# Half 1's last feed-forward tile issued product by product between matmuls of half 0's second product

## The chip, the cores and the metric

One Trainium2 chip, one of its cores. The metric is the device time of one execution in microseconds (us), the median of several runs.

## The reference, cut to what matters

One step of a hybrid decoder trunk in f32: a half-step SwiGLU feed-forward, a token mixer (pooling, Mamba-2), a second half-step feed-forward and a norm. 1024 prompt tokens and 64 sample tokens share all weights; D_MODEL is 1024, D_FF 2816.

```python
def swiglu(x, w_in, w_out):
    gu = x @ w_in
    g, u = gu[..., :D_FF], gu[..., D_FF:]
    return (jax.nn.silu(g) * u) @ w_out

x = x + 0.5 * swiglu(rmsnorm(x, norm_ffn1), ffn1_w_in, ffn1_w_out)
...
x = x + 0.5 * swiglu(rmsnorm(x, norm_ffn2), ffn2_w_in, ffn2_w_out)
```

## The kernel before

**Halves and tiles.** The tokens are worked on in two halves: half 0 has 512, half 1 has 576 (`NTOK`, line 31). A feed-forward's first product makes the hidden layer in 22 tiles of 128 rows (`NFF`). A hidden tile of a half is stored to DRAM (`hd0` to `hd21` in a trace, for each half) and reloaded for the second product, which makes eight output tiles `po` per half out of all 22.

**Split numbers.** f32 is multiplied as a sum of products of rounded parts. ACT writes the rounded part of a tile, DVE subtracts it from the tile and writes the rest; the page's "split" is such a pair. For a weight they are `wh` (L457) and `wl` (L458), for a reloaded hidden tile `hh` or `hp` (L353) and `hr` or `hp` (L355). TensorE (PE) then does three products of parts for each pair of tiles; for half 0 in the first product it does two, since one wider tile holds both parts of the activations.

**Products of the first half of a feed-forward.** Most hidden tiles are made in Strassen-Winograd form: seven products of half-size blocks in the place of eight. `wino` (L481) runs over `PRODUCTS`, in the order 1, 2, 6, 5, 7, 3, 4. Their weights come from `wino_weights` (L442): four raw blocks a11, a12, a21, a22 (loaded by `wino_raw`, L472, DMA at L477, tag `wraw` with six buffers), and four sums of them, which POOL makes at L451: s1 = a21 + a22, s2 = s1 - a11, s3 = a11 - a21, s4 = a12 - s2. They are split in the order a11, a12, s2, s1, s3, s4, a22, with three buffers each for `wh` and `wl`. What PE has accumulated in PSUM (`pw` in a trace) goes out by `after0` for half 0 (L555 on, with POOL's half sums at L567 and its product at L588) and by `after` for half 1 (L591 on, POOL's product at L618): copies by ACT, sums by DVE, a SiLU by ACT. The next product in a bank waits for the copy of the last.

**The order of the work.** `ffn` (L640) makes the tiles up to `NFF - N_APART` with each weight used for both halves. The last one, tile 21, is made apart: for half 0, then for half 1, each with weights of its own, loaded and split anew (L668 to L670). The second product follows, half 0 first: the 22 hidden tiles are loaded at L685 and split, output tiles 0 and 1 are accumulated together and then the others one by one. In a trace these matmuls are `po<-hh`, `po<-hr` and `po<-hp`. The weights of output tiles 0 and 1 have been split long before and lie in DRAM as halves `part`; `load_w` reloads them at L282 into `wh` and `wl`, every other pair into two of the six `wraw` buffers.

The program text doesn't set the order on the engines alone. A tile scheduler gives each instruction a place by its priority and by a model of durations, and work that runs beside a stream of matmuls is written as a chain: a generator that `start` registers, and that `tick`, called after each group of matmuls, moves on one step when the modelled PE time since its last step has passed the number that it yielded. `finish` runs a chain to its end. What stands in each engine's queue is fixed when the program is built, and each engine works its queue in that order. All loads and stores here are issued by SP (SyncE) from one queue, so that one that waits holds those behind it. PE's matmuls are all at L164.

Of the kernel before, what the change touches and what calls it, by code (L numbers as in the profile page):

```python
# [14 lines left out]
P = 128  # L15
D = 1024
KD = D // P
FF = 2816
# [17 lines left out]
N_ACT, N_PAIR, N_BIG, N_PD = 42, 8, 3, 4  # L36
N_RAW, N_W = 6, 3
N_FX, N_S, N_PDF = 17, 4, 6
N_PLAIN, N_APART = (3, 2), 1

PRODUCTS = (("1", 0), ("2", 1), ("6", 0), ("5", 2), ("7", 0), ("3", 2), ("4", 0))

# [20 lines left out]
def tile_hybrid_pool_ssd_macaron(  # L63
# [71 lines left out]
    def start(gen, delay=0.0):  # L135
        c = Chain(gen, delay)
        chains.append(c)
        return c
# [17 lines left out]
    def tick():  # L156
        while chains:
            c = min(chains, key=lambda q: q.due)
            if c.due > pe[0]:
                return  # L160
            c.step()
# [318 lines left out]

    def wino(weights, nk, xs, after):  # L481


        banks = [[None] * 3 for _ in xs]
        for (p, b), (wh, wl) in zip(PRODUCTS, weights):
            for i, (h, X) in enumerate(xs):
                n = NPAIR[h]
                new = banks[i][b] is None
                if new:
                    banks[i][b] = psum("pd", "pw" + p)  # L490
                out = banks[i][b][:, :n]
                if h == 0:
                    both = banks[i][b].rearrange("p (a b) -> p a b", a=2)
                    for k in range(nk):
                        x = X[p][k]
                        mm(both, wh[:, k, :], x, start=new and k == 0, stop=False, free=True)
                        mm(out, wl[:, k, :], x[:, 0, :], start=False, stop=k == nk - 1, free=True)
                    after(p, i, banks[i])
                    tick()
                    continue  # L500
                for k in range(nk):
                    xh, xl = X[p][k]
                    for j, (W, x) in enumerate(((wh, xh), (wh, xl), (wl, xh))):
                        mm(out, W[:, k, :], x, start=new and k == 0 and j == 0, stop=k == nk - 1 and j == 2, free=True)
                after(p, i, banks[i])
                tick()

    def combine(h, xn, hi, lo, hl, X, pace):

# [38 lines left out]
                X["4"][i] = hl[i][:, :, s_]  # L548
            yield pace

    def ffn_in(wi, ff, xs):

        out = {}

        def after0(p, i, bk):  # L555

            A, B, C = bk
            n = NPAIR[0]
            f, s_ = slice(0, n), slice(n, 2 * n)
            if p == "1":  # L560
                out[i] = o = {"g": fx(name="g"), "t": fx(name="t"), "v": fx(name="v")}
                S.copy(o["t"][:, : 2 * n], A)
                return
            g, t, v = out[i]["g"], out[i]["t"], out[i]["v"]

            def halves(o, x):
                G.tensor_tensor(o, x[:, f], x[:, s_], op=ALU.add)  # L567

            if p == "2":
                V.tensor_tensor(g[:, : 2 * n], B, t[:, : 2 * n], op=ALU.add)  # L570
                halves(g[:, f], g)
                S.activation(g[:, f], g[:, f], AF.Silu)
            elif p == "6":
                S.copy(v[:, : 2 * n], A)  # L574
            elif p == "5":
                S.copy(t[:, : 2 * n], C)
            elif p == "7":
                V.tensor_tensor(t[:, : 2 * n], A, t[:, : 2 * n], op=ALU.add)  # L578
                halves(t[:, f], t)
            elif p == "3":  # L580
                V.tensor_tensor(v[:, : 2 * n], C, v[:, : 2 * n], op=ALU.add)
                halves(g[:, s_], v)
                S.activation(g[:, s_], g[:, s_], AF.Silu)
            else:
                S.copy(t[:, s_], A[:, s_])
                V.tensor_tensor(t[:, s_], A[:, f], t[:, s_], op=ALU.add)
                V.tensor_tensor(g[:, f], g[:, f], t[:, s_], op=ALU.mult)
                G.tensor_tensor(g[:, s_], g[:, s_], t[:, f], op=ALU.mult)  # L588
                dma(hdram[0][ff], g[:, : 2 * n])

        def after(p, i, bk):  # L591
            h = xs[i][0]
            if h == 0:
                return after0(p, i, bk)
            n = NPAIR[h]
            A, B, C = (b[:, :n] if b is not None else None for b in bk)
            if p == "1":
                t = fx(name="t")
                out[i] = o = {"g": fx(name="g"), "t1": t[:, :n], "t5": t[:, :n], "t2": t[:, n : 2 * n]}
                S.copy(o["t1"], A)  # L600
                return
            o = out[i]
            g1, g2 = o["g"][:, :n], o["g"][:, n : 2 * n]
            if p == "2":
                V.tensor_tensor(g1, B, o["t1"], op=ALU.add)
                S.activation(g1, g1, AF.Silu)
            elif p == "6":
                S.copy(o["t2"], A)
            elif p == "5":
                S.copy(o["t5"], C)  # L610
            elif p == "7":
                V.tensor_tensor(o["t5"], A, o["t5"], op=ALU.add)
            elif p == "3":
                V.tensor_tensor(g2, C, o["t2"], op=ALU.add)
                S.activation(g2, g2, AF.Silu)
            else:
                V.tensor_tensor(g1, g1, A, op=ALU.mult)
                G.tensor_tensor(g2, g2, o["t5"], op=ALU.mult)  # L618
                dma(hdram[h][ff], o["g"][:, : 2 * n])

        wino(wino_weights(wi, 0, 4, 4, ff * P, FF + ff * P), 4, xs, after)

    def ffn_in_plain(wi, ff, x):

# [14 lines left out]
    def ffn(wi, wo, prep, after, half=None, side=None):  # L639

        X, todo, behind = [{}, {}], [], []
        for h in HALVES:
            finish(prep[h][0])
            x = prep[h][1][0]
            gen = combine(h, x[3], x[1], x[2], x[4], X[h], T_PACE)

            def first(gen):
                for p in gen:  # L650
                    if p is None:
                        return
                    yield p

            c = start(first(gen), T_AT)
            for ff in range(N_PLAIN[h]):
                ffn_in_plain(wi, ff, x[:3])
            todo.append(c)
            behind.append(start(rest(c, gen)))
        for c in behind:  # L660
            finish(c)
        if side:
            side = start(side, PART_AT)
        for ff in range(N_PLAIN[1], N_PLAIN[0]):
            ffn_in(wi, ff, [(1, X[1])])
        for ff in range(N_PLAIN[0], NFF - N_APART):
            ffn_in(wi, ff, [(h, X[h]) for h in HALVES])
        for h in HALVES:  # L668
            for ff in range(NFF - N_APART, NFF):
                ffn_in(wi, ff, [(h, X[h])])  # L670
        if side:
            finish(side)
        for h in HALVES:
            N = NTOK[h]
            parts = [], []
            for k in range(NFF):

                own = k < 4 if h == 0 else not half and k >= NFF - 2
                if 4 <= k < 4 + N_PAIR and (h == 0 or half):
                    a, t, _ = pair(576, "hp")  # L680
                    t = t.bitcast(F32)
                else:
                    t, a = (fx(d, n_) if own else act((P, 576), d, n_) for d, n_ in ((F32, "hr"), (F32R, "hh")))
                t = t[:, :N]
                dma(t, hdram[h][k])  # L685
                split(t, a[:, :N], t.bitcast(F32R))
                parts[0].append(a)
                parts[1].append(t.bitcast(F32R))
            xt = []
            for ms in ((0, 1),) + tuple((m,) for m in range(2, KD)):  # L690
                po = [banks([(h,)], "pd", "po")[0] for _ in ms]
                for kb in range(0, NFF, 4):
                    n4 = min(4, NFF - kb)
                    for m, pts in zip(ms, po):
                        wh, wl = load_w(wo, kb, n4, m * P)
                        for kk in range(n4):
                            products([pts], wh, wl, kk, slice(0, P), [(h, *parts)], kb + kk, NFF)
                            tick()
                for m, pts in zip(ms, po):
                    x_ = fx(name="x")  # L700
                    dma(x_[:, :N], xspill[h][m])
                    for pt, (a, b) in zip(pts, PIECES[h]):
                        V.scalar_tensor_tensor(x_[:, a:b], pt[:, : b - a], 0.5, x_[:, a:b], op0=ALU.mult, op1=ALU.add)
                    xt.append(x_)
                if half and ms[-1] == KD // 2 - 1:
                    half(h, xt)
            after(h, xt)
# [904 lines left out]
```

## Time and profile before

| | |
|---|---|
| runs | 2926.48, 2932.68, 2932.84 us |
| median of the runs | 2932.68 us |
| profiled execution | 2926.27 us |
| its span | 2924.5 us |
| granted PE clock, mean | 0.998 |
| PE busy | 98% |
| DVE / ACT / POOL busy | 58% / 41% / 18% |
| DMA, mean | 171 GB/s |

The profile shows one execution. Its span runs from the first to the last instruction that it has recorded, and the time of the execution is 1.8 us longer. Rows of the timeline give the start, the duration, the engine, the line, what is written and read, and in brackets the engine's idle time before the instruction and what released it. PE, DVE (VectorE), ACT (ScalarE), POOL (GpSimd) and SP are the engines, PEld is PE's loading of weights. The passage from the first product to the second is at about 495 to 533 us in the first feed-forward and at 2611 to 2649 us in the second.

### The profile page before, as it was taken

The page shows a single profiled execution, that of the slowest core. Times are in us where ns is not written, and L with a number is a line of the kernel's source. Part 1 is how long each engine was busy: PE and PEld are TensorE (multiplying, and loading weights), DVE is VectorE, ACT ScalarE, POOL GpSimd, SP SyncE. Part 2 cuts the span into 40 slices and gives each one's busy share as a digit, 9 for nine tenths or more (in the row PEclk, how much of TensorE's full clock was granted, in tenths as well). Part 3 has the DMA queues.
Part 4 walks back from the last instruction along what each step waited for, and adds up shares of the span by engine and source line. Part 5 has one row for each costly group of instructions (what it writes and reads, how often), then busy time and mean ns, then how long its engine had stood idle before and what let it go on. Part 6 is the DMA issues. An engine that isn't in the chain of part 4 may idle for free.

```text
span 2924.5 us, 50164 instructions
## 1 busy us (share of the span) xinstructions
PE 2873.3 (98%) x18622; PEld 2621.2 (90%) x18622; DVE 1706.2 (58%) x3172; ACT 1208.9 (41%) x2456; POOL 533.3 (18%) x642
## 2 busy tenths in 40 slices
PE   7999999999999999999999999999999999999998
PEld 6999999789988888788999989999999999987898
DVE  6665555434273897787643786867666554453432
ACT  5444444323242655443332554443233444443422
POOL 6444444000000000000000010100035444440000
PEclk9999999999999999999999999999999999999999
DMA  4575554854335878678434566556574532236652
GB/s 135 166 227 181 161 173 131 283 188 145 101 97 164 281 254 265 205 226 280 129 98 148 170 187 185 168 165 186 177 244 154 162 98 78 82 103 210 216 161 73
DMA packets 542266, 501.23 MB, mean 171 GB/s; under 512 B 36388, under 2 KB 391780, under 8 KB 542014
## 3 DMA queue, kind: packets, MB, share of 16 engines
q1 hardware_dynamic: 542006, 498.03, 54.4%
q8 instruction: 146, 2.39, 0.3%
q14 instruction: 98, 0.80, 0.1%
q10 hardware_dynamic: 16, 0.00, 0.0%
HBM read 355.94 MB, written 142.20 MB: 170 GB/s over the span
## 4 chain that ended last, share of the span: by engine, by line
PE 90%; DMA 4%; DVE 3%; ACT 1%; issue 1%; POOL 1%; SPq 0%; POOLq 0%; ACTq 0%; DVEq 0%
PE pw L164 26%; PE po L164 18%; PE pc L164 9%; PE pg L164 8%; PE pz L164 7%; PE pu L164 5%; PE pso L164 5%; PE pbp L164 3%; PE pwo L164 3%; PE pyd L164 1%; PE pst L164 1%; PE pyo L164 1%; DMA bsel<-in_bsel_dram 1%; PE pgm L164 1%; DMA hr<-hd 1%
## 5 line engine op out<-in xcount | busy, mean ns | idle before, releaser
L293 DVE TENSOR_TENSOR wl<-wraw,wh 128x512 fp32r<-128x512 f32 (+1 forms) x416 | 284.4, 685 | 409.2 <-ACT wh L292 396.0
L292 ACT ACTIVATE wh<-wraw 128x512 fp32r<-128x512 f32 (+1 forms) x416 | 257.4, 620 | 617.6 <-PE po L164 248.7
L164 PE MATMUL pw<-X,wh 128*128 128x288 f32 (+1 forms) x1416 | 353.9, 329 | 5.3 <-ACT v L574 3.5
L164 PE MATMUL pw<-X,wl 128*128 128x288 f32 (+1 forms) x936 | 268.6, 287 | 0.0
L164 PEld LDWEIGHTS pw<-X,wh 128*128 128x128 f32 x1416 | 237.6, 188 | 27.3 <-ACT v L574 4.2
L164 PE MATMUL pc<-hl,wh 128*128 128x288 f32 (+1 forms) x1152 | 256.6, 331 | 0.0
L164 PE MATMUL pw<-hl,wh 128*128 128x512 f32 x608 | 219.5, 396 | 1.1 <-DVE t L578 1.0
L458 DVE TENSOR_TENSOR wl<-s,wh 128x512 fp32r<-128x512 f32 x168 | 131.9, 785 | 144.4 <-ACT wh L457 122.8
L164 PE MATMUL po<-hh,wh 128*128 128x288 f32 (+1 forms) x800 | 210.4, 323 | 3.5 <-ACT hh L353 2.5
L164 PE MATMUL po<-hr,wh 128*128 128x288 f32 (+1 forms) x800 | 210.6, 322 | 0.1
L164 PE MATMUL po<-hh,wl 128*128 128x288 f32 (+1 forms) x800 | 210.0, 322 | 0.0
L164 PE MATMUL pg<-hl,wh 128*128 128x288 f32 (+1 forms) x864 | 201.7, 338 | 0.8 <-issue 0.8
L164 PEld LDWEIGHTS pc<-hl,wh 128*128 128x128 f32 x1152 | 184.5, 188 | 18.1 <-issue 3.5
L164 PE MATMUL pw<-hi,wh 128*128 128x288 f32 x640 | 189.1, 296 | 0.6 <-ACT t L610 0.6
L164 PE MATMUL pw<-hi,wl 128*128 128x288 f32 x640 | 188.4, 294 | 0.0
L164 PE MATMUL pw<-lo,wh 128*128 128x288 f32 x640 | 188.4, 294 | 0.0
L164 PEld LDWEIGHTS pw<-X,wl 128*128 128x128 f32 x936 | 176.5, 189 | 0.0
L164 PE MATMUL pz<-hl,wh 128*128 128x288 f32 (+1 forms) x768 | 174.4, 335 | 0.0
L164 PE MATMUL pw<-hl,wl 128*128 128x256 f32 x608 | 169.2, 278 | 0.0
L164 PE MATMUL pc<-hl,wl 128*128 128x288 f32 (+1 forms) x576 | 158.2, 328 | 0.0
L164 PEld LDWEIGHTS pg<-hl,wh 128*128 128x128 f32 x864 | 141.3, 189 | 15.7 <-issue 2.5
L458 DVE TENSOR_TENSOR wl<-wraw,wh 128x512 fp32r<-128x512 f32 x126 | 103.2, 819 | 87.5 <-ACT wh L457 81.0
(375 smaller groups left out, 6872.7 us busy)
## 6 DMA issues: line engine op xcount, KB each, us to landing
wh<-part SPq DMA_DIRECT2D x204, 256.0 KB
wl<-part SPq DMA_DIRECT2D x204, 256.0 KB
wraw<-in_ffn_w_in_dram SPq DMA_DIRECT2D x188, 256.0 KB
wraw<-in_w_in_dram SPq DMA_DIRECT2D x180, 256.0 KB
wraw<-in_ffn_w_out_dram SPq DMA_DIRECT2D x120, 256.0 KB
part<-wh SPq DMA_DIRECT2D x112, 256.0 KB
part<-wl SPq DMA_DIRECT2D x112, 256.0 KB
ab<-acsd SPq DMA_DIRECT2D x64, 256.0 KB
```

Source lines behind the costliest of these rows:

```text
L164: T.matmul(out, lhsT, rhs, start=start, stop=stop, skip_group_check=free)
L292: S.activation(wh, raw, AF.Copy)
L293: V.tensor_tensor(wl, raw, wh.bitcast(F32), op=ALU.subtract)
L458: V.tensor_tensor(wl, a, wh.bitcast(F32), op=ALU.subtract)
```

## The change

Half 0's tile 21 is made as before. Half 1's becomes a chain, `behind`, that is started after it and moves on one product per step while the second product of half 0 is being issued, each step 1.3 us of modelled PE time after the last (`APART_PACE`); what is left of it is issued behind output tiles 0 and 1. For this, `wino` is turned into a generator, `wino_steps`, that yields after each product. The matmuls, splits, sums and transfers are the same in number.

```diff
-N_PLAIN, N_APART = (3, 2), 1
+N_PLAIN, N_APART, APART_PACE = (3, 2), 1, 1.3
...
     def wino(weights, nk, xs, after):
+        for _ in wino_steps(weights, nk, xs, after):
+            tick()
+
+    def wino_steps(weights, nk, xs, after):
...
                     after(p, i, banks[i])
-                    tick()
+                    yield
                     continue
...
                 after(p, i, banks[i])
-                tick()
+                yield
...
-    def ffn_in(wi, ff, xs):
+    def ffn_in(wi, ff, xs, apart=False):
...
-        wino(wino_weights(wi, 0, 4, 4, ff * P, FF + ff * P), 4, xs, after)
+        steps = wino_steps(wino_weights(wi, 0, 4, 4, ff * P, FF + ff * P), 4, xs, after)
+        if apart:
+            return steps
+        for _ in steps:
+            tick()
...
-        for h in HALVES:
+        for ff in range(NFF - N_APART, NFF):
+            ffn_in(wi, ff, [(0, X[0])])
+
+        def behind():
             for ff in range(NFF - N_APART, NFF):
-                ffn_in(wi, ff, [(h, X[h])])
+                for _ in ffn_in(wi, ff, [(1, X[1])], apart=True):
+                    yield APART_PACE
+
+        apart = start(behind())
         if side:
             finish(side)
...
                     xt.append(x_)
+                if h == 0:
+                    finish(apart)
                 if half and ms[-1] == KD // 2 - 1:
                     half(h, xt)
```

The rows below are from the passage of the first feed-forward; the one of the second reads alike. In names the numbers are those of buffers and of the program's counter; lines behind 480 are some lines later in the changed kernel.

PE, before: behind half 0's tile (`pw_1134_5887`) come the seven products of half 1's tile, 84 matmuls, and then `po`. The rows are the end of half 0's tile and the beginning of half 1's.

```order
L164 MATMUL pw_1134_5887<-hl_311,wl_5981 128x256
L164 MATMUL pw_1162_6009<-hi_437,wh_6005 128x288
L164 MATMUL pw_1162_6009<-lo_438,wh_6005 128x288
L164 MATMUL pw_1162_6009<-hi_437,wl_6006 128x288
L164 MATMUL pw_1162_6009<-hi_450,wh_6005 128x288
```

PE, with the change, at the same place and then further on, inside product 5 (weights `wh_6176`, `wl_6177`):

```order
L164 MATMUL pw_1134_5887<-hl_311,wl_5981 128x256
L164 MATMUL po_6099<-hh_5998,wh_6101 128x512
L164 MATMUL po_6099<-hr_5997,wh_6101 128x512
L164 MATMUL po_6099<-hh_5998,wl_6103 128x512
L164 MATMUL pw_1202_6120<-hi_437,wh_6116 128x288
...
L164 MATMUL pw_1214_6180<-X_814,wh_6176 128x288 x2
L164 MATMUL po_6099<-hh_6003,wh_6101 128x512
L164 MATMUL po_6099<-hr_6002,wh_6101 128x512
L164 MATMUL po_6099<-hh_6003,wl_6103 128x512
L164 MATMUL po_6099<-hh_6008,wh_6101 128x512
```

Three `po` matmuls stand ahead of product 1, six inside product 5 and five behind product 6; products 1 and 2, and products 7, 3 and 4, follow each other without `po` between.

POOL, before: the sums of half 1's weights (`s`, s1 to s4) stand around the first half sum of half 0's tile (`g_5896`, `t_5897`).

```order
L451 TENSOR_TENSOR s_1168_6044<-wraw_6001,wraw_6003 128x512
L451 TENSOR_TENSOR s_1169_6046<-s_1168_6044,wraw_5997 128x512
L567 TENSOR_TENSOR g_5896<-g_5896 128x256
L451 TENSOR_TENSOR s_1175_6083<-wraw_5997,wraw_6001 128x512
L451 TENSOR_TENSOR s_1178_6102<-wraw_5999,s_1169_6046 128x512
L567 TENSOR_TENSOR t_5897<-t_5897 128x256
L567 TENSOR_TENSOR g_5896<-v_5898 128x256
L588 TENSOR_TENSOR g_5896<-g_5896,t_5897 128x256
```

POOL, with the change:

```order
L571 TENSOR_TENSOR g_5896<-g_5896 128x256
L571 TENSOR_TENSOR t_5897<-t_5897 128x256
L571 TENSOR_TENSOR g_5896<-v_5898 128x256
L451 TENSOR_TENSOR s_1208_6155<-wraw_6112,wraw_6114 128x512
L451 TENSOR_TENSOR s_1209_6157<-s_1208_6155,wraw_6108 128x512
L592 TENSOR_TENSOR g_5896<-g_5896,t_5897 128x256
L451 TENSOR_TENSOR s_1215_6194<-wraw_6108,wraw_6112 128x512
L451 TENSOR_TENSOR s_1218_6213<-wraw_6110,s_1209_6157 128x512
```

All four sums moved behind the three half sums, two of them ahead of the product that finishes half 0's tile.

DVE, before: the last instructions up to the split of half 1's last raw weight (`wl_6123`), the eighteenth from the split of its first.

```order
L458 TENSOR_TENSOR wl_6086<-s_1175_6083,wh_6085 128x512
L355 TENSOR_TENSOR hp_6169<-hp_6169 128x512
L458 TENSOR_TENSOR wl_6105<-s_1178_6102,wh_6104 128x512
L355 TENSOR_TENSOR hp_6173<-hp_6173 128x512
L355 TENSOR_TENSOR hp_6177<-hp_6177 128x512
L458 TENSOR_TENSOR wl_6123<-wraw_6003,wh_6122 128x512
```

DVE, with the change, from the split of s3 (`s_1215_6194`) to that of the last raw weight (`wl_6234`), now the twenty-sixth:

```order
L458 TENSOR_TENSOR wl_6197<-s_1215_6194,wh_6196 128x512
L355 TENSOR_TENSOR hr_6012<-hr_6012,hh_6013 128x512
L355 TENSOR_TENSOR hp_6037<-hp_6037 128x512
L355 TENSOR_TENSOR hp_6041<-hp_6041 128x512
L609 TENSOR_TENSOR g_6134<-pw_1207_6140,t_6133 128x288
L355 TENSOR_TENSOR hp_6045<-hp_6045 128x512
L458 TENSOR_TENSOR wl_6216<-s_1218_6213,wh_6215 128x512
L355 TENSOR_TENSOR hr_6064<-hr_6064,hh_6065 128x512
L458 TENSOR_TENSOR wl_6234<-wraw_6114,wh_6233 128x512
```

Fifteen splits of reloaded hidden tiles stand between the first and the last weight split of half 1's tile, where there were seven. ACT's queue changes in the same way; there the copy of half 1's product 1 (L600, now L604) stands behind the split of the reload `hr_6012`.

SP, with the change: the loads and stores from the first `po` weight half to the reload behind half 0's store.

```order
L282 DMA wl_6103<-part_1521 128x512
L477 DMA wraw_6108<-in_ffn_w_in_dram 128x4x128
L477 DMA wraw_6110<-in_ffn_w_in_dram 128x4x128
L477 DMA wraw_6112<-in_ffn_w_in_dram 128x4x128
...
L699 DMA hr_6059<-hd_14_135 128x512
L477 DMA wraw_6114<-in_ffn_w_in_dram 128x4x128
L699 DMA hr_6002<-hd_1_122 128x512
...
L593 DMA hd_21_142<-g_5896 128x512
L699 DMA hp_6033<-hd_8_129 128x512
L699 DMA hr_6012<-hd_3_124 128x512
```

Before, the four raw loads (L477) stood ahead of the first two `part` halves (L282), and the store of half 0's tile 21 (`hd_21_142`, L589) ahead of the reload of hidden tile 0; now two `part` halves stand ahead of the raws, the fourth raw stands behind three reloads, and the store behind the reloads of tiles 0, 1, 2, 4 to 7, 13 and 14.

## The prediction

> **What bounds the kernel now.** I read the page first, then the busy time in stretches around the two places that the change touches, then single rows on each engine there.
>
> ```profile
> span 2924.5 us, 50164 instructions
> PE 2873.3 (98%) x18622; PEld 2621.2 (90%) x18622; DVE 1706.2 (58%) x3172; ACT 1208.9 (41%) x2456; POOL 533.3 (18%) x642
> PE 90%; DMA 4%; DVE 3%; ACT 1%; issue 1%; POOL 1%; SPq 0%; POOLq 0%; ACTq 0%; DVEq 0%
> ```
>
> PE is busy for 98% of the span and holds 90% of the chain that ended last. A change can gain only where PE stands still, and loses where it makes PE stand. The change touches the passage from a feed-forward's first product to its second, once in each feed-forward. The stretches (busy us of each engine, granted clock, DMA share, GB/s) show those passages and what follows them:
>
> ```profile
> 507.00:533.00 26.00, 23.37 (x133) 19.18 (x134) 21.60 (x34) 17.00 (x34) 5.93 (x5) 1.00 0.88 298
> 533.00:560.00 27.00, 27.00 (x120) 22.33 (x119) 6.14 (x9) 4.43 (x7) 0.00 (x0) 1.00 0.83 270
> 2620.00:2649.00 29.00, 24.57 (x142) 20.09 (x140) 22.95 (x35) 18.49 (x37) 8.77 (x9) 1.00 0.81 272
> 2649.00:2680.00 31.00, 31.00 (x138) 25.58 (x137) 7.39 (x11) 5.63 (x9) 0.00 (x0) 1.00 0.77 251
> ```
>
> In the first row PE (first number) stands for 2.6 of 26 us while DVE (third) is busy for 21.6, so DVE has 4.4 us to spare; right behind, PE has no gap at all and DVE is nearly idle. Two things follow. A shift at the passage goes one to one into the end, since PE has no gap behind it to take it up. And inside the passage the engine next to full is DVE. The second feed-forward reads the same. PE's rows (start, duration, idle before and releaser):
>
> ```profile
> 507.16 0.50 PE L164 MATMUL pw<-X,wh 128*128 128x512 f32 x1 [1.78 <-ACT v L574]
> 511.56 0.30 PE L164 MATMUL pw<-hi,wh 128*128 128x288 f32 x1
> 511.69 0.29 PE L164 MATMUL pw<-lo,wh 128*128 128x288 f32 x1
> 515.64 0.40 PE L164 MATMUL pw<-X,wh 128*128 128x288 f32 x1 [0.76 <-ACT t L600]
> 525.76 0.50 PE L164 MATMUL po<-hh,wh 128*128 128x512 f32 x1 [0.86 <-DMA wh<-part]
> 531.00 0.50 PE L164 MATMUL po<-hh,wh 128*128 128x512 f32 x1 [0.74 <-ACT hh L353]
> 532.54 0.40 PE L164 MATMUL po<-hh,wl 128*128 128x512 f32 x1
> 532.78 0.40 PE L164 MATMUL po<-hp,wh 128*128 128x512 f32 x1
> 2622.98 0.50 PE L164 MATMUL pw<-X,wh 128*128 128x512 f32 x1 [1.74 <-ACT v L574]
> 2631.49 0.40 PE L164 MATMUL pw<-X,wh 128*128 128x288 f32 x1 [0.76 <-ACT t L600]
> 2647.00 0.73 PE L164 MATMUL po<-hh,wh 128*128 128x512 f32 x2 [1.78 <-ACT hh L353]
> ```
>
> Half 1's tile begins at 511.56 and the first reloaded pair tile (`hp`) is used at 532.78: 21.2 us for 84 `pw` matmuls and 24 `po` matmuls. Starts lie 0.13 us apart for `pw` (511.56, 511.69) and 0.23 for `po` (532.54, 532.78 is 0.24), so the work is 84 x 0.132 + 24 x 0.2275 = 11.1 + 5.5 = 16.6 us. **About 4.6 us per passage are lost**, the visible waits and small ones between; they are the most that the interleaving can win there, with 0.74 more from below. The second feed-forward has its three waits of nearly the same size (1.74, 0.76, 1.78) in the same places, and the order of the work there is the same. I work out the first and double it.
>
> **The change, step by step.** No matmul, split, sum or transfer is added or taken away; the instructions of half 1's tile go behind others on every engine.
>
> *Step 1, half 0's tile ends earlier.* POOL's sums for half 1's weights no longer stand ahead of half 0's own half-sum:
>
> ```profile
> 502.99 0.68 DVE L570 TENSOR_TENSOR g<-pw,t 128x512 f32<-128x512 f32 x1
> 503.19 1.29 POOL L451 TENSOR_TENSOR s<-s,wraw 128x512 f32<-128x512 f32 x1 [0.68 <-POOL s L451]
> 504.44 1.18 POOL L567 TENSOR_TENSOR g<-g 128x256 f32<-128x256 f32 x1
> 505.66 0.42 ACT L572 ACTIVATE g<-g 128x256 f32<-128x256 f32 x1 [2.58 <-POOL g L567]
> 506.54 0.57 ACT L574 COPY v<-pw 128x512 f32<-128x512 f32 x1
> ```
>
> DVE has `g` ready at 503.67, POOL begins at 504.44 because the sum runs until then, the SiLU follows at 505.66, the copy of `v` behind it, and PE's 1.78 us wait ends. Without the sum ahead it all comes 0.74 us earlier (0.77 from 503.67, less a start). **Gain 0.74**; half 0's tile ends at 510.8.
>
> *Step 2, the sums meet DVE's splits.* Now the four sums run in about 512 to 521, where DVE is next to full. What they then cost, from the rows of before:
>
> ```profile
> 503.59 1.45 DVE L458 TENSOR_TENSOR wl<-s,wh 128x512 fp32r<-128x512 f32 x1
> 505.58 1.27 POOL L451 TENSOR_TENSOR s<-wraw,wraw 128x512 f32<-128x512 f32 x1
> 507.55 1.30 POOL L451 TENSOR_TENSOR s<-wraw,s 128x512 f32<-128x512 f32 x1 [0.70 <-POOL s L451]
> 507.67 1.72 DVE L458 TENSOR_TENSOR wl<-wraw,wh 128x512 fp32r<-128x512 f32 x1 [0.26 <-ACT wh L457]
> 509.92 0.68 DVE L458 TENSOR_TENSOR wl<-wraw,wh 128x512 fp32r<-128x512 f32 x1
> 517.65 0.68 DVE L458 TENSOR_TENSOR wl<-s,wh 128x512 fp32r<-128x512 f32 x1
> 520.66 0.68 DVE L458 TENSOR_TENSOR wl<-wraw,wh 128x512 fp32r<-128x512 f32 x1
> ```
>
> A split alone takes 0.68 us. The one that met the sum at 503.19 took 1.45, the one that met that at 507.55 took 1.72: 0.77 and 1.04 more, and each ended about 0.5 us after the sum did. A split that is ready when the sum begins would lose the sum's whole 1.29. For a queue with work waiting I take 1.15, between 1.04 and 1.29: four sums cost 4.6 us. The ends are nothing (the sums fall beside DVE's reads of PSUM or its idle time) and 4 x 1.29 = 5.2. The Trainium skill, "SBUF — State Buffer", section "Who interferes with whom", says that a DVE instruction with two SBUF inputs and a GpSimd instruction that reads SBUF exclude each other for the whole of whichever came first. The two pairs of rows agree (1.45 and 1.72 for 0.68). By the rule to the letter the sum below would come out at +3.6 per passage, and with splits untouched by the sums at rival 1.
>
> *Step 3, more splits stand ahead of half 1's last weight.* On DVE the splits from the tile's first weight (509.92) to its last (520.66) were the first and last of 18 instructions, 17 starts in 10.74 us, 0.632 each, with 7 splits of reloaded tiles among them. Now there are 26 with 15. DVE begins 0.74 earlier, at 509.2: 25 x 0.632 = 15.8, and 4.6 for the sums. What it idles for its own inputs I take from two groups of 500 to 535:
>
> ```profile
> L458 DVE TENSOR_TENSOR wl<-s,wh 128x512 fp32r<-128x512 f32 x8 | 6.8, 853 | 2.5 <-ACT wh L457 2.5
> L355 DVE TENSOR_TENSOR hr<-hr,hh 128x512 fp32r<-128x512 f32 x10 | 7.8, 796 | 5.0 <-ACT hh L353 5.0
> ```
>
> That is 0.31 us per weight split, or 0.5 per split of a reloaded tile. I take 0.31 for the six weight splits that follow the first, 1.9 us; the ends are nothing and 6 x 0.5 = 3.0. So the last split starts at 509.2 + 15.8 + 4.6 + 1.9 = 531.5 and ends at 532.2. Ten of product 4's twelve matmuls follow it (1.3 us, 533.5), and then those ten of the 24 `po` matmuls that aren't spread between the products (10 x 0.2275 = 2.3): 535.8, where before the same 108 matmuls were done at 532.78. **Loss 3.0 us per passage**, step 1's gain inside it. PE is in order, so its own work (510.8 + 16.6 = 527.4 without a gap) is no bound here.
>
> *Step 4, SP.* The raw weights of half 1's tile went out in four places, the last three from this row:
>
> ```profile
> 488.44 7.00 SPq L477 DMA_DIRECT2D wraw<-in_ffn_w_in_dram  x3
> ```
>
> Two halves of prepared `po` weights now go ahead of half 1's raw weights, taking two of the six buffers; the first three raws come one place later, which still is over 8 us ahead of their use, and the fourth, which had gone out by 495.4, waits for half 0's last weight split. That ended at 509.39 (507.67 + 1.72); 0.74 earlier and with no sum beside it (1.04 less), it ends at 507.6. A transfer of this size landed 2.22 to 4.11 us after its issue (rows below), so the raw is there at 510 to 512, when the first sum needs it; that sets the sums at the place where step 2 has them. In exchange the wait of 0.86 for `wh<-part` goes; it is part of the 4.6 us lost before, and step 3's end at 535.8 takes that into account. The store of half 0's tile now waits for a product on POOL behind two sums, and two reloads are queued behind that store (rows of the timeline; those of DMA are from the chain of work, issue to landing):
>
> ```profile
> 514.07 1.21 POOL L588 TENSOR_TENSOR g<-g,t 128x256 f32<-128x256 f32 x1 [0.53 <-ACT g L583]
> 516.22 0.32 SPq L589 DMA_DIRECT2D hd<-g  x1
> 500.30 2.22 DMA hd<-g
> 518.04 4.79 DMA hr<-hd
> 525.54 4.11 DMA hr<-hd
> 520.57 0.65 ACT L353 ACTIVATE hh<-hr 128x512 fp32r<-128x512 f32 x1
> 515.20 0.39 ACT L600 COPY t<-pw 128x288 f32<-128x288 f32 x1
> ```
>
> Two sums are 2.6 us, less 0.7 of step 1 and 0.5 that POOL idled: store at 517.6, the reload of the fourth tile at 518.4, landed after 4.11 to 4.79 at 522.5 to 523.2, split by ACT (0.63), then the copy of product 1 (0.39), which product 6 has to wait for and which is queued behind that split: 523.5 to 524.2. From there to the end of the 108 come 50 `pw` and 15 `po` matmuls, 6.6 + 3.4 = 10.0 us: 533.5 to 534.2. That lies below 535.8, so DVE decides and this chain is second, 1.6 us or more behind.
>
> **The sum.** Two passages at +3.0 are +6.0 us. The profiled execution took 2926.27 us around its span of 2924.5; that makes 2932.3. The three runs have a median of 2932.68, 6.4 above the profiled execution, and the forecast for such a median is **2938.7**, 0.2% slower.
>
> **The rivals.**
>
> *Rival 1, not slower: DVE isn't held.* If the sums fall beside DVE's PSUM reads and its idle time, step 3 ends 4.6 us earlier, below the chain of step 4, which then decides. With the reload landing in between 2.22 and 4.11 us (3.2) and POOL's product taking 0.5 less, it ends at 532.1, **-0.7 per passage**, 2931.3. It decides if at most one of the four sums holds a split. For it speaks that the sum at 505.58 met no split (DVE stood idle beside it); against it that DVE's 21.6 us of 26 leave little room.
>
> *Rival 2, a heavier loss: DVE idles at the head of its queue.* If weight splits wait for ACT's halves, because ACT has hh and hp splits ahead of them and a wait for a reload holds everything behind it, the dear ends hold: 5.2 for 4.6 and 3.0 for 1.9, **+4.7 per passage**, +9.4, 2942.1. It decides where DVE's idle time before weight splits passes 3 us per passage. The DMA share of 0.88 speaks for it (a reload landed 4.79 us after its issue).
>
> *Rival 3, the passage closes.* PE runs 16.6 us without a gap from 510.8: 527.4, -5.4 per passage, 2922.0. That needs DVE to give the last weight by 524, with 25 instructions at 0.59 and nothing held; no row of the passage gives that pace.
>
> *Rival 4, the change does nothing:* the products could come out in the old order. The order on PE excludes it: 14 `po` matmuls stand between half 1's products, and ten more behind.
>
> **Chances.** Forecast 0.47; rival 1 0.25; rival 2 0.23; rival 3 0.05; rival 4 none. What a measurement of this kernel can tell from no change is about 0.3%, 8.8 us. Faster by more: rival 3 nearly whole, 0.04. Slower by more: rival 2 and a little of the forecast's upper end, 0.27. Within: 0.69. The range goes from 2927 (rival 1 with the fastest of the three runs in mind, 2926.48) to 2944 (rival 2 and a bit); it leaves out rival 3 and the ends of rivals 1 and 2, about 0.15.
>
> **What would show it.** Step 1: PE's wait of 1.78 at half 0's sixth product shrinks to about 1.0. Step 2: splits of 1.3 to 1.9 us on DVE beside the four sums, at 512 to 521. Step 3: the last weight's split ends near 532, PE waits for DVE or for ACT's `wh` inside products 5, 6 and 3, and the 108 matmuls end some 3 us later after half 0's tile than before. Rival 1 would show splits of 0.68 beside the sums and PE waiting for the copy of product 1. It would be wrong altogether if PE's work behind the passage had gaps that take up the shift, or if DVE's instructions behind 533 ran late enough to hold the `po` products.

## The result, and the profile after

| | before | with the change |
|---|---|---|
| median, 18 runs each | 2928.69 us | 2935.20 us |
| profiled execution | 2926.27 us | 2935.27 us |
| its span | 2924.5 us | 2933.5 us |
| granted PE clock, mean | 0.998 | 0.996 |

The kernel is **slower by 0.23%**: the ratio to before is 1.0023, 95% interval 1.0016 to 1.0031, or 6.7 us, and 6.5 us between the medians. Forecast were 6.0 us. The forecast time of 2938.7 lies 3.5 us above the measured one because it stood on a median of three runs before, which 18 runs put 4 us lower.

A passage is measured here from one fixed point, the start of POOL's last product of tile 20 (`g<-g,t 128x288`), to the end of the 108 matmuls (84 of half 1's tile, 24 of the second product). These are PE's waits and POOL's fixed point with the change, first feed-forward, then second:

```profile
499.29 1.10 POOL L622 TENSOR_TENSOR g<-g,t 128x288 f32<-128x288 f32 x1
507.17 0.50 PE L164 MATMUL pw<-X,wh 128*128 128x512 f32 x1 [0.71 <-ACT v L578]
511.50 0.40 PE L164 MATMUL po<-hh,wh 128*128 128x512 f32 x1
515.49 0.40 PE L164 MATMUL pw<-hi,wl 128*128 128x288 f32 x1 [1.27 <-DVE wl L458]
518.34 0.52 PE L164 MATMUL pw<-X,wh 128*128 128x288 f32 x2 [1.26 <-ACT wh L457]
520.42 0.50 PE L164 MATMUL po<-hh,wh 128*128 128x512 f32 x1 [0.88 <-ACT hh L353]
523.24 0.79 PE L164 MATMUL po<-hr,wh 128*128 128x512 f32 x1 [2.31 <-DVE hr L355]
531.36 0.54 PE L164 MATMUL pw<-X,wh 128*128 128x288 f32 x2 [0.21 <-ACT t L612]
538.62 0.39 PE L164 MATMUL po<-hr,wh 128*128 128x512 f32 x1
2618.61 1.10 POOL L622 TENSOR_TENSOR g<-g,t 128x288 f32<-128x288 f32 x1
2642.50 0.72 PE L164 MATMUL po<-hr,wh 128*128 128x512 f32 x1 [2.31 <-DVE hr L355]
2657.37 0.39 PE L164 MATMUL po<-hr,wh 128*128 128x512 f32 x1
```

The matmuls at 538.62 and 2657.37 are the 109th. From the fixed point that is 39.3 and 38.8 us; before it was 34.6 and 34.75 (fixed points 498.16 and 2614.02, 109th matmuls at 532.78 and 2648.77). So **the two passages lost 4.7 and 4.0 us** in these two executions. Their profiled times lie 9.0 us apart, where the medians differ by 6.5, so these sizes are a little large for the medians. The rows of before that the prediction doesn't show:

```profile
498.16 1.09 POOL L618 TENSOR_TENSOR g<-g,t 128x288 f32<-128x288 f32 x1
2614.02 1.10 POOL L618 TENSOR_TENSOR g<-g,t 128x288 f32<-128x288 f32 x1
2648.77 0.63 PE L164 MATMUL po<-hp,wh 128*128 128x512 f32 x2
```

The same part by stretches (PE, PEld, DVE, ACT, POOL busy, then the granted clock, DMA share, GB/s):

```profile
513.00:518.00 5.00, 2.80 (x20) 2.34 (x18) 5.00 (x6) 2.33 (x5) 4.92 (x5) 1.00 0.54 180
518.00:523.00 5.00, 1.71 (x6) 0.93 (x6) 5.00 (x6) 4.32 (x9) 2.83 (x2) 0.99 0.84 266
523.00:529.00 6.00, 5.76 (x21) 5.06 (x22) 5.36 (x10) 1.86 (x3) 0.00 (x0) 0.50 0.71 263
529.00:533.00 4.00, 3.79 (x22) 3.23 (x22) 1.99 (x3) 3.12 (x7) 0.00 (x0) 0.90 0.36 101
```

Two things are to be seen. From 513 to 523 DVE is busy throughout, but only with 12 instructions, and PE works for 4.5 of 10 us. Then, from 523 to 529, PE is busy and does only 21 matmuls: its granted clock is 0.50. The second feed-forward shows the same, shorter (0.50 from 2643 to 2646). DVE and POOL in the first two of these stretches, with one row of ACT:

```profile
513.15 1.73 POOL L451 TENSOR_TENSOR s<-wraw,wraw 128x512 f32<-128x512 f32 x1
514.00 1.43 DVE L458 TENSOR_TENSOR wl<-wraw,wh 128x512 fp32r<-128x512 f32 x1
514.96 1.62 POOL L451 TENSOR_TENSOR s<-s,wraw 128x512 f32<-128x512 f32 x1
515.36 1.50 DVE L591 TENSOR_TENSOR g<-g,t 128x256 f32<-128x256 f32 x1
516.61 0.63 ACT L457 ACTIVATE wh<-s 128x512 fp32r<-128x512 f32 x1 [2.44 <-POOL s L451]
517.41 1.73 POOL L451 TENSOR_TENSOR s<-wraw,wraw 128x512 f32<-128x512 f32 x1
517.92 1.77 DVE L355 TENSOR_TENSOR hp<-hp 128x512 fp32r<-128x512 f32 x1
519.11 1.72 POOL L451 TENSOR_TENSOR s<-wraw,s 128x512 f32<-128x512 f32 x1
519.62 1.76 DVE L458 TENSOR_TENSOR wl<-s,wh 128x512 fp32r<-128x512 f32 x1
522.50 0.68 DVE L355 TENSOR_TENSOR hr<-hr,hh 128x512 fp32r<-128x512 f32 x1
```

Each of the four sums holds one DVE instruction: 1.43, 1.77 and 1.76 us for splits of 0.68, and 1.50 for a product of 0.41. That is 0.75 + 1.09 + 1.09 + 1.08 = 4.0 us. The sums are held too: 1.62 to 1.73 us instead of 1.29. They also come late: ACT stands for 2.44 us until the second sum is there, and what is queued on ACT behind that `wh` stands with it. The split at 522.50 is the one that PE waits 2.31 us for, at 523.24.

### The profile page after: what moved, and what is told of

Read it like the earlier page. It is cut to its first block, busy times and chain, and to the rows that moved or that the text cites. A ratio compares the mean times of both kernels' runs of the same rounds, so it can differ in the third digit from the quotient of the medians.

```text
span 2933.5 us, 50170 instructions
## 1 busy us (share of the span) xinstructions
PE 2877.8 (98%) x18622; PEld 2625.4 (89%) x18622; DVE 1709.7 (58%) x3172; ACT 1206.4 (41%) x2456; POOL 533.4 (18%) x642
## 4 chain that ended last, share of the span: by engine, by line
PE 92%; DVE 3%; DMA 2%; ACT 1%; issue 1%; POOL 0%; SPq 0%; POOLq 0%; ACTq 0%; DVEq 0%
PE pw L164 26%; PE po L164 17%; PE pc L164 10%; PE pg L164 8%; PE pz L164 7%; PE pso L164 6%; PE pu L164 5%; PE pbp L164 3%; PE pwo L164 3%; PE pyd L164 1%; PE pst L164 1%; PE pyo L164 1%; PE pgm L164 1%; PE pxT L168 1%; DMA xin<-in_x_prompt_dram 0%
```

## The experiments

The theory at this point, **A**: the POOL sums, moved into a stretch where DVE is full, hold DVE's splits; PE waits for the late splits, one of the waits is so long that PE's clock is halved, and that makes the passage longer still. The rivals: **B**, the chain of reloads behind half 0's late store on SP sets the passage; **C**, the greater number of reload splits ahead of the last weight is the cost, whatever the sums do; **D**, the halved clock costs nothing by itself.

### Raw weights requested first (e_raws)

```diff
+        raws = wino_raw(wi, 0, 4, 4, (NFF - 1) * P, FF + (NFF - 1) * P)
         def behind():
             for ff in range(NFF - N_APART, NFF):
-                for _ in ffn_in(wi, ff, [(1, X[1])], apart=True):
+                for _ in ffn_in(wi, ff, [(1, X[1])], apart=True, raws=raws):
```

> The change, with the four raw weight blocks of half 1's last tile requested right behind half 0's tile, ahead of the second product's loads. By the order of the queues this brings the four POOL sums back to where they stood before the change (two ahead of half 0's first half sum), while PE's interleaving and the fifteen reload splits ahead of the last weight split on DVE stay as in the change. Theory A (the sums hold DVE's splits, PE then waits so long that its clock is halved): the splits beside 512 to 521 take 0.68 us again, the last weight split ends about 4 us earlier (near 528), no stretch of the passage has a granted clock under 0.9, each passage is 0.5 to 1 us shorter than before the change, ratio to before 0.9994 (0.998 to 1.0005). Rival B (the chain of reloads behind half 0's store on SP sets the passage): that chain is not touched, the ratio stays at 1.0015 to 1.0025. Rival C (the fifteen splits ahead are the whole cost): 1.002.

Measured: ratio to before **1.0002** (0.9994 to 1.0011), 2929.94 us. The passage by stretches:

```profile
513.00:518.00 5.00, 4.36 (x30) 3.91 (x29) 5.00 (x8) 3.83 (x9) 2.61 (x3) 1.00 0.95 314
518.00:523.00 5.00, 3.24 (x16) 2.02 (x16) 5.00 (x9) 4.11 (x8) 0.00 (x0) 1.00 0.83 260
523.00:529.00 6.00, 6.00 (x38) 5.20 (x38) 5.49 (x10) 4.70 (x11) 0.00 (x0) 1.00 1.00 363
529.00:533.00 4.00, 4.00 (x32) 3.95 (x31) 1.62 (x5) 1.19 (x3) 0.62 (x1) 1.00 0.72 244
```

and two of the four weight splits of half 1's tile from sums, with PE's longest waits there:

```profile
520.05 0.68 DVE L458 TENSOR_TENSOR wl<-s,wh 128x512 fp32r<-128x512 f32 x1
521.86 0.68 DVE L458 TENSOR_TENSOR wl<-s,wh 128x512 fp32r<-128x512 f32 x1
...
520.28 0.49 PE L164 MATMUL po<-hh,wh 128*128 128x512 f32 x1 [0.68 <-ACT hh L353]
521.39 0.50 PE L164 MATMUL po<-hr,wh 128*128 128x512 f32 x1 [0.61 <-DVE hr L355]
534.51 0.47 PE L164 MATMUL po<-hh,wh 128*128 128x512 f32 x1 [0.90 <-DMA wh<-part]
```

POOL does nothing from 518 to 529, DVE does 17 instructions in the ten microseconds in which it did 12, the splits shown take 0.68 us again, and the clock is 1.00 throughout this passage. In the second passage it isn't. It is 0.50 for 3.4 us from 2641.1, behind waits of 0.48, 0.79 and 0.47 us, which gives this mean over four microseconds:

```profile
2641.00:2645.00 4.00, 4.00 (x21) 4.00 (x20) 3.66 (x7) 1.90 (x4) 0.00 (x0) 0.57 1.01 367
```

So A's forecast that no stretch falls under 0.9 failed there, and its size was too good: from the fixed point the passages take 35.0 and 35.6 us, 0.3 and 0.8 us more than before, not 0.5 to 1 us less. New waits of 0.5 to 0.9 us (for `hh`, `hr`, `wl` and `wh<-part`) stand where the old ones were (0.76, 0.86, 0.74).

By the ratio the interleaving costs nothing any more that these runs can tell. The same fifteen reload splits stand ahead of the last weight split, and PE's order is of the same kind (18 `po` matmuls ahead of the last of half 1's products, where the change has 14), so C falls as the main cost. The sums still hold splits of DVE where they now stand, three of them (1.28, 1.45 and 1.72 us, as before the change), but there DVE has room. B isn't settled by this run: in SP's queue the reloads behind the store are where they were, but the store goes out 4.7 us after half 0's tile and no longer 6.0, since no sum stands ahead of POOL's product.

### The sums on DVE (e_dve)

```diff
-                G.tensor_tensor(t, a, b, op=op)
+                (eng or G).tensor_tensor(t, a, b, op=op)
...
-                for _ in ffn_in(wi, ff, [(1, X[1])], apart=True):
+                for _ in ffn_in(wi, ff, [(1, X[1])], apart=True, eng=V):
```

> The change, with the four sums of half 1's last tile made by DVE in the place of POOL. Theory A: a sum costs DVE its own 0.68 us or less instead of the 1.0 to 1.1 us by which it holds a split; thirty starts at 0.632 from 509.2 and 1.9 of waits put the last weight split at 530.1 in the place of 531.5, 1.4 us less per passage, so +1.6 per passage and a ratio to before of 1.0011 (1.0003 to 1.0018). Half 0's store goes out about 2.6 us earlier since no sum stands ahead of its product on POOL. Rival B (reload chain behind the store): the earlier store gives back 2 to 3 us per passage, ratio 0.9995 to 1.0005. Rival C (any instruction more on DVE ahead of the last weight costs): four more instructions, +2.5 per passage on top of the change, ratio 1.004.

Measured: ratio **1.0016** (1.0007 to 1.0024), 2932.87 us, within A's range, at its upper end. The sums now hold nothing, but they are late: ACT stands for 1.16 us until the second is there, and the split of a reload (`hh`) that is queued behind it is the one for which PE waits 2.32 us. PE's clock falls again, for 6.8 us in each passage. The row of ACT, and the stretches:

```profile
521.35 0.63 ACT L457 ACTIVATE wh<-s 128x512 fp32r<-128x512 f32 x1 [1.16 <-DVE s L451]
```

```profile
518.00:523.00 5.00, 1.84 (x6) 0.78 (x5) 5.00 (x10) 2.65 (x6) 0.00 (x0) 0.88 0.94 311
523.00:526.00 3.00, 2.75 (x9) 2.06 (x9) 3.00 (x6) 2.92 (x7) 0.00 (x0) 0.50 0.68 193
```

From the fixed point the passages take 36.7 and 37.3 us, 2.1 and 2.6 more than before. That fits the account of A: a sum costs DVE 1.0 us where it holds a split and 0.68 where DVE makes it. The intervals of this run and of the change overlap, so the times alone don't show the gain. The run also shows that the lock (a sum on POOL and a split on DVE holding each other) is not the whole of it: sums made here, on whichever engine, come late for ACT and for the products that need them. B falls here: the store goes out 3.9 us after half 0's tile, 2.0 us sooner than in the change, and the ratio is above the 0.9995 to 1.0005 that B gave. C's 1.004 is excluded too.

### PE kept busy in its longest wait (e_fill)

```diff
-                            products([pts], wh, wl, kk, slice(0, P), [(h, *parts)], kb + kk, NFF)
+                            fill = h == 0 and ms[0] == 0 and m == 0 and kb + kk == 2
+                            with tc.high_priority(400 if fill else 0):
+                                if fill:
+                                    for _ in range(10):
+                                        T.matmul(po[1][0], wh[:, 0, :], parts[0][0][:, :512], start=True, stop=False, skip_group_check=True)
+                                products([pts], wh, wl, kk, slice(0, P), [(h, *parts)], kb + kk, NFF)
```

The raised priority puts the fill inside product 5.

> The change, with ten idle-fill matmuls on PE (2.3 us at full clock) ahead of the reload tile 1's products inside product 5; they write a PSUM bank that is begun anew later, so nothing that is computed changes. They can only fill time in which PE waited in the change's profile (0.88 and 2.31 us before tile 2's products). Theory A': the half clock (0.50 for 523 to 529.5 in the first passage, 2642.8 to 2645.5 in the second) comes from PE's little work in the 3 to 10 us before; with the fill the granted clock stays at 1.0, products 5 and 6 keep 0.13 us a matmul in the place of 0.24, and up to 3.2 and 1.9 us come back: ratio to before 1.0006 to 1.0015. If the last weight split on DVE binds all the same, only the lower half of it: 1.0015. Rival D (the half clock is not the passage's loss, or doesn't come from PE's idling): ratio as in the change or above, 1.0023 to 1.003.

Measured: ratio **1.0016** (1.0007 to 1.0026), 2932.79 us, 2.4 us below the change's median though PE does 4.6 us more work. The intervals of the two ratios overlap, so the times alone don't settle D; the trace does. The splits on DVE are held as in the change, and the clock is halved in neither passage:

```profile
518.00:523.00 5.00, 3.77 (x16) 2.82 (x16) 5.00 (x6) 4.07 (x9) 2.70 (x2) 1.00 0.87 288
523.00:529.00 6.00, 5.42 (x32) 4.50 (x33) 6.00 (x12) 4.12 (x9) 0.00 (x0) 1.00 0.68 246
```

PE does 32 matmuls in 523 to 529 instead of 21. Product 5 can go on when the rest of its weight (`wl`) has been split, and that is 25.2 us after the fixed point in both kernels. These are the first of the 22 matmuls of half 1 from there and the `po` behind the last, in e_fill and then in the change:

```profile
524.31 0.40 PE L164 MATMUL pw<-X,wl 128*128 128x288 f32 x1 [0.47 <-DVE wl L458]
527.36 0.40 PE L164 MATMUL po<-hh,wh 128*128 128x512 f32 x1
```

```profile
524.44 0.61 PE L164 MATMUL pw<-X,wl 128*128 128x288 f32 x1
529.84 0.39 PE L164 MATMUL po<-hh,wh 128*128 128x512 f32 x1
```

They take 3.05 us instead of 5.40, and 3.04 instead of 4.08 in the second passage: the half clock stretched them by 2.35 and 1.04 us. Leaving the fill out of the count, the 109th matmul comes 37.9 and 38.1 us after the fixed point, 1.4 and 0.6 us sooner than in the change. What is won is partly lost again, to waits of 1.02 and 1.22 us for `wh<-part`, of which the change has only one, of 0.39 us. The profiles are typical in this: the mean granted clock of all executions is 0.9949 with the change, 0.9972 in e_fill and 0.9969 in the 27 executions of the kernel before that were run beside f_s13. D falls; the clock is a part of the loss, 2.0 of 8.7 us in the profiles and, less surely, 2.4 of 6.5 us between the medians.

### s3 ahead of the half sum in the place of s2 (f_s13)

e_raws, with the four sums issued at once, in another order:

```diff
+        for o, a, b, op in ((t[0], a21, a22, ALU.add), (t[1], a11, a21, ALU.subtract),
+                            (t[2], t[0], a11, ALU.subtract), (t[3], a12, t[2], ALU.subtract)):
+            G.tensor_tensor(o, a, b, op=op)
```

> The run with the raw weights requested first (e_raws), with the four sums made at once and in the order s1, s3, s2, s4, so that s3 and no longer s2 stands ahead of half 0's first half sum on POOL. s3 needs nothing of s1 and so doesn't wait the 0.68 us between the two. Theory A: the half sum begins about 0.6 us earlier, PE's wait of 1.78 us for the copy of v shrinks to about 1.2, and that is all: 0.6 us per passage, ratio to before 0.9998 (0.999 to 1.0006), since e_raws stood at 1.0002. Rival: the passage ends by DVE's splits or by the reloads all the same, and the gain is taken back by later waits: 1.0002, with the 108 matmuls ended no earlier than in e_raws.

Measured: ratio **1.0006** (0.9997 to 1.0014), 2930.63 us; PE's wait for `v` is 1.73 us. The sum s3 has to wait for a buffer instead ("0.63 <-DVE wl"), so that the half sum comes no sooner. The intervals of this run and e_raws overlap: nothing gained that these runs can tell, as the rival said.

### Longer steps between the products (f_p26, f_p39, f_s13p26)

e_raws with `APART_PACE` 2.6 and 3.9 in the place of 1.3, and f_s13 with 2.6.

> e_raws with steps of 2.6 us of modelled PE time between half 1's products in the place of 1.3, so that about twice as many matmuls of the second product stand between them. Theory A says that what is left in e_raws are waits for splits of reloaded tiles (0.64, 0.68, 0.61, 0.47 us) and for one reload (0.90); half 1's products, whose operands are there, then fill such waits for longer: up to 1.3 us per passage, ratio to before 0.9995 (0.9985 to 1.0005). Rival C (each split of a reloaded tile ahead of the last weight split costs 0.63 us of DVE): later weights, 1 to 2 us per passage slower than e_raws, ratio 1.001 to 1.0015.

> The same with 3.9 us. Theory A: as at 2.6 or a little better, 0.9992 to 1.0002, since the wait of 0.90 us for the second pair of prepared weights then has half 1's products to fill it. Rival C: worse again, 1.0015 to 1.0025.

> f_s13 and f_p26 together. Theory A: the two gains are of different waits and add up, ratio 0.9991 (0.998 to 1.0002), the first version of the interleaving that is no slower than the kernel before. Rivals: as in f_p26.

Measured: **1.0009** (1.0000 to 1.0018), **1.0035** (1.0023 to 1.0048) and **1.0005** (0.9996 to 1.0014). That half 1's products fill the remaining waits was wrong. With 3.9 the kernel is slower than e_raws; between 1.3 and 2.6 the intervals overlap. (39 and 75 `po` matmuls stand ahead of the last of half 1's products, 18 in e_raws.) PE's waits with 3.9, from the timeline, and the stretches beside them:

```profile
523.70 0.79 PE L164 MATMUL po<-hh,wh 128*128 128x512 f32 x1 [2.75 <-ACT hh L353]
527.19 0.85 PE L164 MATMUL pw<-X,wh 128*128 128x288 f32 x2 [0.69 <-ACT wh L457]
```

```profile
518.00:523.00 5.00, 1.77 (x5) 0.48 (x3) 3.39 (x6) 2.12 (x4) 0.00 (x0) 0.75 0.97 294
523.00:526.00 3.00, 2.30 (x5) 1.45 (x5) 1.60 (x3) 2.49 (x5) 0.00 (x0) 0.50 1.00 370
526.00:530.00 4.00, 3.31 (x11) 2.52 (x10) 2.79 (x5) 2.29 (x5) 0.00 (x0) 0.50 0.70 264
```

Rival C's sizes lie inside the intervals or at their edge, but its mechanism isn't there: DVE is busy for 3.4 of 5 and 1.6 of 3 us, no longer full. PE waits for `hh`, ACT's split of a reload, ACT waits for the reloads (1.36, 0.55 and 0.98 us in a row behind 518.9), and the DMA share is 0.97 to 1.00. Matmuls of the second product that are moved ahead need their reloads sooner than the DMA queues deliver them, and PE, in order, has half 1's products queued behind them. How much of the loss is the clock, 0.50 for 10.2 us in each passage, is not parted here.

### A fifth buffer for the sums (b_ns5, r_ns5)

The kernel before, and e_raws, each with

```diff
-N_FX, N_S, N_PDF = 17, 4, 6
+N_FX, N_S, N_PDF = 16, 5, 6
```

> The kernel before, without the interleaving, with five buffers for the weight sums in the place of four and sixteen in the place of seventeen for the f32 tiles of the first stage. In every run so far but the change, POOL's first sum waits about 1.97 us for a weight split that frees its buffer, and the sums then stand in the way of half 0's half sum. With a fifth buffer s1 can start right after the product ahead of it, and s1, s2 and s3 are done about when half 0's g is. Theory A: PE's waits of 1.78 and 1.74 us for the copy of v shrink by 0.7 to 1.0 each, as they did in the change (0.71, 0.64 left), without the lock's cost later, so 1.4 to 2 us in all: ratio 0.9994 (0.9987 to 1.0003). Rival: PE waits later for the same reloads and weights, the gain is taken back: 1.0000; or the missing f32 tile delays stores: 1.0005.

> e_raws (interleaving, raw weights requested first) with the same five and sixteen buffers. Theory A: 1.4 to 2 us less than e_raws (1.0002), ratio 0.9996 (0.9988 to 1.0005), which would not tell it from the kernel before with five buffers. If the interleaving is worth anything once the lock is out of the way, it lies below the kernel before with five buffers by more than 0.0005; if not, on it or above.

Measured: **1.0005** (0.9996 to 1.0013) and **1.0003** (0.9994 to 1.0012). The expected gain didn't come: in the first passage s1 now waits for its raw weights (1.90 us) and stands ahead of POOL's last product of tile 20, and PE's wait for `v` grew to 2.69 and 2.64 us. The sums still hold splits there (two of them take 2.56 us in b_ns5). But the pair answers the other question: where the sums are early, with and without the interleaving are the same to what these runs can tell, here as in e_raws against the kernel before. No version here beats the kernel before.

## Why the prediction was right

The direction, the size and the first cause were right; that the size came so near is in part luck. By its own steps:

- **What bounds it**: right. Behind the passage PE has no gap, and what a passage loses arrives at the end: 8.7 us in the two, 9.0 between the executions.
- **Step 1, half 0's tile ends 0.74 us earlier**: 1.2 us in both passages (511.50 is 12.2 us behind the fixed point, 511.56 was 13.4). PE's wait of 1.78 became 0.71, where 1.0 was forecast. The rest comes from the lock as well: with the sums gone from there, the split ahead of `g` on DVE took 0.69 us and no longer 1.28, which the step had left out.
- **Step 2, the sums hold DVE's splits for 4.6 us**: 4.0 us, at 513 to 521, as forecast. Run e_raws shows that the sums in this stretch are what the change costs: with the raw weights early and the sums back where they were, 1.0023 becomes 1.0002. The rule weighed there (the Trainium skill, "SBUF — State Buffer", section "Who interferes with whom") holds for each of the four pairs of rows: each DVE instruction ends 0.5 to 0.6 us after the sum beside it, the short product 0.3. Its value to the letter, 5.2 us, is further off than the one estimated from rows. What the runs do not part is the hold on DVE from the lateness of the sums: ACT stands for 2.44 us until POOL has the second sum at 516.6, and the `wh` for which PE waits 1.26 us is queued behind that. The fourth raw weight was requested only at 508.39. e_raws takes hold and lateness away together; e_dve takes the hold away, gives DVE the sums to make, and keeps 2.1 and 2.6 of the 4.7 and 4.0 us.
- **Step 3, the last weight split sets the end**: the sum was near, the place was wrong. That split started at 531.87, 32.6 us behind the fixed point (forecast 33.3), but PE wasn't waiting for it. What set PE was the split of the third reload (522.50), 1.3 us of work behind the last held split in DVE's queue: PE waited 2.31 us for it, and from there on, in the first passage, for nothing longer than 0.21. DVE even stood still for 1.84 us later, since ACT's half of a weight waited 3.38 us for PE to give back a buffer. The "own inputs" of 1.9 us came out near (2.2, the 1.84 and 0.38 ahead of the last split) for another reason than the one given.
- **Not foreseen: the clock.** The matmuls behind that wait ran at 0.50, and this is the term that the sum lacks: 3.0 per passage were forecast, 4.7 and 4.0 measured in the profiled execution. In e_fill, where the same splits are held and the clock is 1.00, the passages lose 3.3 and 3.4 us against before. The clock's share is the other 1.4 and 0.6 us.
- **Step 4, SP**: the chain behind half 0's store stayed second, as forecast, but by less. The store went out at 517.48, in an execution that stands 1.1 us later at that place, so 1.2 us sooner than forecast, and the copy of product 1 behind its reload was done at 522.78, 0.46 us before PE's long wait ended. That DVE and not this chain decides rests on the row of that wait (`<-DVE hr`) and on e_dve, where the store is 2.0 us sooner and PE still waits 2.32 us.
- **Rival 1**: its condition, at most one sum that holds a split, wasn't met: three of the sums held a split and the fourth a product. e_raws, with no sum in this stretch, comes nearest to it, and its passages are 0.3 and 0.8 us longer than before, where -0.7 was given. **Rival 2** had the right size for the first passage (4.7) by luck: it asked for more than 3 us of idle time before DVE's weight splits, 2.2 were measured, and a part of the loss was the clock. Rivals 3 and 4 didn't come about.

The forecast of 6.0 us lies near the 6.5 between the medians although the sum has no clock in it and ends on a split for which PE didn't wait. What carries it is step 2. Open is how the loss divides between the hold on DVE and the lateness of the sums.

## What to carry to other kernels

Before work is interleaved to fill one engine's waits, look at which engine is next to full there, and at every helper instruction that moves along: here four POOL sums went from a stretch in which DVE had room into one in which it had none, and each held a DVE instruction for about 1 us. A matmul that is moved ahead asks for its operands sooner; if PE works in order and the reloads come at the rate of a full DMA queue, as in f_p39, the products ahead of the second product were the time in which its operands arrived. And a wait of PE is to be priced with what can follow it: the wait of 2.31 us here took the clock with it, which cost another 1.4 and 0.6 us, while one of 2.64 us in r_ns5 did not.

## What the runs showed of the hardware

The granted clock of PE fell to 0.50 after short waits: after 2.31 us in both passages of the change, after 2.69 us in b_ns5, for 3.4 or 6.8 us. The length alone doesn't decide: r_ns5 waited 2.64 us at the same place and stayed at 1.00, e_raws fell in its second passage with no wait longer than 0.79 us near, and f_p26 fell to 0.50 (511 to 513) after a wait of 1.78 us, as long as that before the change, where it stayed at 1.00. In the 3.41 us right ahead of the fall PE had worked for 0.51 us in the first passage of the change, 1.45 in b_ns5, 1.63 in f_p26 and 1.71 in e_raws; how much work is enough to keep the clock these runs don't tell. These rows show PE's clock, microsecond by microsecond, in b_ns5 (wait to 509.16) and in r_ns5 (wait to 510.35):

```profile
508.00:509.00 1.00, 0.00 (x0) 0.00 (x0) 0.28 (x1) 1.00 (x3) 0.89 (x1) 0.71 0.75 244
509.00:510.00 1.00, 0.84 (x3) 0.74 (x4) 0.76 (x2) 1.00 (x3) 0.00 (x0) 0.50 0.75 272
514.00:515.00 1.00, 1.00 (x5) 0.81 (x4) 0.92 (x2) 0.53 (x1) 0.06 (x1) 0.50 0.82 272
515.00:516.00 1.00, 1.00 (x7) 0.91 (x6) 1.00 (x3) 0.62 (x2) 0.48 (x1) 0.87 1.04 387
```

```profile
509.00:510.00 1.00, 0.00 (x0) 0.00 (x0) 0.08 (x1) 1.00 (x3) 1.00 (x1) 1.00 0.50 158
510.00:511.00 1.00, 0.65 (x3) 0.60 (x4) 0.78 (x2) 1.00 (x3) 0.09 (x1) 1.00 1.00 356
```

The Trainium skill, "TensorE: Matmul & The Clock Gate", section "Part 1: The HAM clock gate (the "warmup" mystery)", says that PE's clock has two levels, one half of the other, and is set by its activity in free-running windows of about 3.4 us. The two levels, the dependence on where a wait falls, and durations of one, two or (f_p39) three such windows agree with that. The Trainium skill's table there gives at least one idle window as the condition of the fall. Read as a window in which PE does nothing, that doesn't agree, since PE worked in the 3.41 us ahead of each of these falls and no wait in the passages was longer than 2.75 us.
